# Nine instead of eight feed-forward chunks as seven products, and the sums T1 and T3 of the weights formed by accumulating loads

## The chip, the cores and the metric

The kernel runs on one core of a Trainium2 chip. The metric is the device time of one execution in microseconds. Before the change it is 2186.28 us, the median of three runs (2185.25 to 2186.5).

## The reference

One layer of a hybrid encoder for 256 tokens of width 2048, all in float32:

```
x = LN1(alpha*x + 0.5*(silu(x@w1) * (x@w3)) @ w2)          # feed-forward 1, D_FF = 5632
x = LN2(alpha*x + mixer(x))                                # projections w_in, mLSTM (4 heads), stick-breaking
                                                           # attention (8 heads), two gated up-projections, w_out
x = LN3(alpha*x + 0.5*(silu(x@w1') * (x@w3')) @ w2')       # feed-forward 2
x = x + sigmoid(x@w_ple_gate) * (p@w_ple_proj)
```

The weights are read from HBM in float32, plain loads of 440.87 MB in all; the work is nearly all in the matrix products.

## The kernel before

**Products.** TensorE takes float32 numbers here as a rounded part and a rest, so every weight tile is split: ScalarE casts the raw tile to the rounded part (`split_one`, L1262), VectorE subtracts it from the raw tile to get the rest (L1266). A raw weight tile is 256 rows by 512 columns, [128, 2, 512], 512 KB. A *unit* is one weight tile against one half of the tokens (128): two row groups times three matmuls of 128x512 (L1316, L1317, L1318), six matmuls in one go. A plain product uses each split for two units, one for each half of the tokens.

**Seven products for eight.** `seven` (L348 to L402) computes a 2x2 block product, two token halves and two weight matrices (w1 and w3 of a chunk, or two column ranges of w_in), with seven block products for eight, each against its own combination of weight tiles. For every four row groups i (four sets to a chunk, since D = 2048) there are four raw tiles: b11, b12, b22 and b21. Product 1 uses b11 itself; product 5 uses T1 = b11 + b12; product 7 uses T3 = b12 + b22; products 6 and 4 use T1 + b22 and further + b21, formed in b11's page. So a set has seven splits of one unit each, and four sums. A sum is formed in one of two ways:

- by VectorE, `plus`, L365: one tensor_tensor over [128, 1024];
- by an accumulating load: GpSimd issues a DMA that reads the second tile from HBM and adds it onto the page of the first. For T1 this is `plus_load`, L371, issued as soon as product 1's split of b11 is done (L1268 to L1270). For T3 it stands in `loads()`, L1239: b22 is added onto b12's page when b12 has landed, long before its split; the load of b12 is moved AHEAD = 3 loads forward for it (L1209).

The last argument of `seven` says for which sets T1 and T3 come by loads. Feed-forward chunks have `(range(4), (3,))`: T1 always, T3 in the last set only. The mixer's five double products (`both7`, L412) have `none = ((), ())`: both by VectorE. The sums of products 6 and 4 are VectorE's always.

**Feed-forward** (`ffn`, L562). The 5632 hidden columns are 11 chunks of 512. Chunks 0, 4 and 8 are plain (`up`: gate with w1, hidden with w3, 32 units); the other eight go through `up7` (28 units). The hidden chunks are transposed and split (`transposed`, L289) and go through `down`: w2 for a list of chunks, four column groups, each group ending with one VectorE addition per token half (L641). `weave` (L165) strews the units of the eight seven-product chunks evenly through the main line of plain gate, hidden and down units; the last two chunks' down passes follow as a tail.

**Mixer** (L1021 to L1130). In the same way the five `both7` products are woven into the main line of projections, with the mLSTM and stick-breaking heads (`stick`, L974) hung in by a planner (`Sched`) with fixed delays. The matmuls of a head take a PSUM bank; the first one of `stick` is at L982, and its bank is one that VectorE's L1012 of an earlier head has to leave first.

**Order and buffers.** The order on every engine is fixed when the program is built. All raw tiles, splits, activations and residuals share one pool of PAGES = 48 pages of 4 KB per partition. `HELD` gives, per stage, how many raw tiles may be loaded ahead and how many splits may be held: (8, 6) in the feed-forward and "wide" stages, (6, 6) where the mixer is woven, (5, 6) in the rest of the mixer. Plain loads go over SyncE's queue (L1234), accumulating loads over GpSimd's, each queue in order; a load waits until its page is free, which is mostly when TensorE has used the split that lay there.

Of the kernel before, what the change touches and what calls it, by code (L numbers as in the profile page):

```python
# [16 lines left out]
D = 2048  # L17
# [5 lines left out]
EPS = 1e-5  # L23
COL = 512

PAGES = 48
TEMP_BUFS = 6


HELD = {"ffn": (8, 6), "mix": (5, 6), "woven": (6, 6), "wide": (8, 6)}  # L30
RAW_EDGE, SPLIT_EDGE = 4, 11
EDGE = 6

# [145 lines left out]
def flat(pairs):  # L179
    return [u for p in pairs for u in p]  # L180
# [7 lines left out]
def kernel(  # L188
# [6 lines left out]
    nc = tc.nc  # L195
# [152 lines left out]
    def seven(wa, ca, wb, cb, rows, cols, act, done, loaded):  # L348

        n = rows // (4 * P)
        accs = {m: {} for m in range(1, 8)}
        accs[2] = accs[1]

        def unit(m, i, tile, src, half, sub):
            return Unit(tile, half, accs[m], src, i, sub, i == 0 and m != 2, i == n - 1,  # L360
                        lambda ps, t, m=m: done(m, ps))

        def plus(out, a, b):
            def make():
                nc.vector.tensor_tensor(out=out.tile[:, :, :cols], in0=a.tile[:, :, :cols], in1=b.tile[:, :, :cols],  # L365
                                        op=ALU.add)
            return make

        def plus_load(out, src):
            def make():  # L370
                nc.gpsimd.dma_start(out=out.tile[:, :, :cols], in_=src, accum_op=ALU.add)  # L371
            return make

        one, rest, then = [], [], []
        for i in range(n):
            b11, b12, b22, b21 = (rows_of(w, (4 * i + sub) * P, c, cols)
                                  for w, c, sub in ((wa, ca, 0), (wb, cb, 0), (wb, cb, 2), (wa, ca, 2)))
            m1 = Weight(b11, [b11], [])
            if i in loaded[0]:
                m5 = Weight(b11, [], [], plus_load(b11, b12.src[0]), m1)  # L380
                m1.soon.append(m5)
            else:
                m5 = Weight(b11, [b12], [], plus(b11, b11, b12), m1)
            if i in loaded[1]:
                assert i in loaded[0]
                b12.plus = b22.src
                m7 = Weight(b12, [b12], [b12])
            else:
                m7 = Weight(b12, [b12, b22] if i in loaded[0] else [b22], [b12], plus(b12, b12, b22),
                            m1 if i in loaded[0] else m5)  # L390
            m6 = Weight(b11, [b22] if i in loaded[1] else [], [], plus(b11, b11, b22), m5)
            m2 = Weight(b21, [], [b21])
            m4 = Weight(b11, [b21], [b11], plus(b11, b11, b21), m6)
            one.append(unit(1, i, m1, act, 0, 0))
            rest.append([unit(5, i, m5, act.forms, 0, 0), unit(7, i, m7, act.forms, 1, 0),
                         unit(6, i, m6, act.forms, 0, 2), unit(3, i, Weight(b22, [], [b22]), act.forms, 1, 2)])
            then += [unit(4, i, m4, act, 1, 2), unit(2, i, m2, act, 0, 2)]
            then[-1].onto = True
        first = []
        for i in range(n):  # L400
            first += one[i + 1:i + 2] + rest[i]
        return one[:1], first, then  # L402

    def in_line(pairs):

        out = []
        for head, first, then in pairs:
            at = max(len(out) - 4, 0)
            out = out[:at] + head + out[at:] + first + then
        return out  # L410
# [151 lines left out]
    def ffn(w1, w3, w2, act, norm, skew=True, ahead=()):  # L562
        n = FF // COL
        hT = ActT(act_tile)

        def turn(src, c, t):
            transposed(src, hT, c, t)
            drop()
            return
            yield  # L570

        def up(c):
            s = {}

            def gate(ps, t):
                s[t] = temp()
                activate(s[t][:], ps, ACT.Silu)

            def hidden(ps, t):
                nc.vector.tensor_tensor(out=s[t][:], in0=ps, in1=s[t][:], op=ALU.mult)  # L580
                sched.spaced(turn(s[t], c, t), DELAY["h"] + 2.0 * t, TURN_GAP)

            return group(w1, range(0, D, 2 * P), c * COL, COL, act, gate), group(w3, range(0, D, 2 * P), c * COL, COL, act, hidden)

        def up7(c):
            r, held = {}, {}

            def both(out, a, b, op):
                nc.vector.tensor_tensor(out=out, in0=a, in1=b, op=op)  # L589

            def done(m, ps):
                held[m] = ps
                if m == 1:
                    r["u"] = temp()
                    nc.scalar.copy(r["u"][:], ps)
                elif m == 2:
                    r["g0"] = temp()
                    activate(r["g0"][:], ps, ACT.Silu)
                    sched.spawn(late(r["u"], r["v"], r["z"], r["g0"]), DELAY["late" if c < n - 1 else "last"])
                elif m == 6:  # L600
                    u, v, z = r["u"], temp(), temp()
                    both(u[:], ps, u[:], ALU.add)
                    both(v[:], held[5], u[:], ALU.add)
                    r["v"], r["z"] = v, z
                    sched.spawn(rest(), DELAY["rest"])
                elif m == 4:
                    sched.until(lambda: "rest" in r)
                    both(r["u"][:], ps, r["u"][:], ALU.add)
                    sched.spawn(silu(r["u"]), DELAY["silu"])
                elif m == 3:  # L610
                    both(r["v"][:], ps, r["v"][:], ALU.subtract)

            def rest():
                both(r["u"][:], held[7], r["u"][:], ALU.add)
                both(r["z"][:], held[5], r["u"][:], ALU.add)
                r["rest"] = True
                return
                yield

            def silu(x):  # L620
                activate(x[:], x[:], ACT.Silu)
                return
                yield

            def late(u, v, z, g0):
                both(v[:], v[:], g0[:], ALU.mult)
                nc.vector.scalar_tensor_tensor(out=z[:], in0=z[:], scalar=-1.0, in1=u[:], op0=ALU.mult, op1=ALU.mult)
                drop(2)
                sched.spaced(turn(v, c, 0), DELAY["h"], TURN_GAP)
                sched.spaced(turn(z, c, 1), DELAY["h"] + 2.0, TURN_GAP)  # L630
                return
                yield

            return seven(w1, c * COL, w3, c * COL, D, COL, act, done, (range(4), (3,)))

        def down(*chunks):
            pairs = []
            for g in range(D // COL):
                def add(ps, t, g=g):
                    xs = xres(t, g * COL)  # L640
                    nc.vector.scalar_tensor_tensor(out=xs, in0=ps, scalar=0.5, in1=xs,  # L641
                                                   op0=ALU.mult, op1=ALU.add)
                    if n - 1 in chunks:
                        norm.chunk(t, g)
                pairs += group(w2, [c * COL + r for c in chunks for r in (0, 2 * P)], g * COL, COL, hT, add)
            return pairs

        gate, hidden = zip(*(up(c) for c in (0, 4, 8)))
        program.extend((skewed(gate[0][:SKEW]) if skew else flat(gate[0][:SKEW])) + flat(gate[0][SKEW:]))
        main = flat(hidden[0] + gate[1] + down(0) + hidden[1] + gate[2] + down(1, 2) + hidden[2] + down(3, 4, 5)  # L650
                    + down(6, 8, 7))
        side = in_line([up7(c) for c in (1, 2, 3, 5, 6, 7, 9, 10)])
        program.extend(main[:HEAD] + weave(main[HEAD:], side))
        program.append(norm.load)
        program.extend(ahead)
        tail = down(9) + down(10)
        program.extend(flat(tail[:-SKEW]) + skewed(tail[-SKEW:]))
        boundary("mix")
# [426 lines left out]
            parts.reverse()  # L1085
        return parts[0] + parts[1]

    none = ((), ())

    def gate_dest(g):  # L1090
        def dest(k, t):
# [10 lines left out]
    gate = branch(0, 1)  # L1102
    main = v(0) + v(1) + sb(8, 9, 2, 3) + sb(10, 11, 4, 5) + [Mode("wide")] + sb(12, 13, 6, 7) + sb(14, 15) + [lambda: sched.spawn(lane())] + branch(0, 0) + gate[:4] + bring_ym_back(gate[4:] + ups(0)) + ups(1) + ups(2)
# [112 lines left out]
    def limits(j):  # L1216

        if at_edge(j):
            return RAW_EDGE, SPLIT_EDGE
        return HELD[[m for e, m in modes if e <= j][-1]]  # L1220

# [132 lines left out]
```

## Time and profile before

| | |
|---|---|
| median of three runs | 2186.28 us |
| the profiled execution's own time | 2185.81 us |
| its span in the profile | 2184.1 us |
| granted TensorE clock, mean | 0.998 |
| TensorE busy | 2169.5 us, 99% |
| VectorE busy | 1925.1 us, 88% |
| ScalarE busy | 1331.5 us, 61% |
| GpSimd busy | 97.2 us, 4% |
| DMA queues: plain loads / accumulating loads | 60.9% / 11.4% of 16 engines |

The span is the time from the first to the last instruction of the program in the profile; the execution's own time has 1.7 us more around it. "Busy" counts an engine as busy while any of its instructions runs; since matmuls are pipelined and overlap, a busy TensorE has to be checked against the distance from one matmul to the next. The feed-forward blocks fill the span from about 0 to 670 us and from about 1420 to 2040 us, the mixer lies between them, and the last product follows.

### The profile page before, as it was taken

Reading aid. Unit: us, or ns where it says so; the run is one execution under the profiler, and the core shown is the slowest. Engines: PE = TensorE matmul, PEld = TensorE weight load, DVE = VectorE, ACT = ScalarE, POOL = GpSimd, SP = SyncE. Lnnn points to the kernel's source line nnn. Section 1 sums busy time; section 2 is a strip of 40 time slices with the busy share of each in tenths; the row PEclk is TensorE's granted clock in tenths of the full one; section 3 lists DMA queues with packets and bytes.
Section 4 is the critical chain, followed back from the end, with each engine's and each line's share of the span. In section 5 each row is a group of like instructions: output and inputs, shape, how many; then the busy total and the mean of one; then the engine's idle time right before and its main releaser. Section 6 shows DMA issues by size and latency. Waiting matters only on the chain. (4 is left out here: it accounts for less than half of the span.)

```text
span 2184.1 us, 27443 instructions
## 1 busy us (share of the span) xinstructions
PE 2169.5 (99%) x9846; PEld 1793.3 (82%) x9846; DVE 1925.1 (88%) x2102; ACT 1331.5 (61%) x1632; POOL 97.2 (4%) x88
## 2 busy tenths in 40 slices
PE   9999999999999999999999999999999999999999
PEld 7888888888888887888878888888888888888887
DVE  6899989999988899898888985799999998999874
ACT  6656565656555765677766564555665655665572
POOL 0010000001000000000000000010001000100000
PEclk9999999999999999999999999999999999999999
DMA  8788788778894755564756686578878878888643
GB/s 320 201 246 244 223 240 250 232 222 253 255 295 139 226 175 174 183 202 143 254 160 221 220 284 212 177 189 252 240 222 237 256 213 230 261 258 259 241 166 103
DMA packets 256521, 484.57 MB, mean 222 GB/s; under 512 B 15576, under 2 KB 32896, under 8 KB 256384
## 3 DMA queue, kind: packets, MB, share of 16 engines
q1 hardware_dynamic: 234624, 440.87, 60.9%
q0 software_dynamic: 21760, 41.95, 11.4%
q8 instruction: 77, 1.26, 0.2%
q14 instruction: 60, 0.49, 0.1%
HBM read 476.47 MB, written 6.29 MB: 221 GB/s over the span
## 5 line engine op out<-in xcount | busy, mean ns | idle before, releaser
L1262 ACT CAST split<-raw 128x1024 fp32r<-128x1024 f32 (+2 forms) x1065 | 1072.2, 1044 | 509.4 <-DVE raw L365 206.8
L1266 DVE TENSOR_TENSOR split<-raw,split 128x1024 fp32r<-128x1024 f32 (+2 forms) x1065 | 1251.7, 1209 | 109.5 <-ACT split L1262 99.4
L1316 PE MATMUL mm<-split,actT 128*128 128x512 f32 (+1 forms) x3080 | 1208.3, 392 | 1.4 <-DVE big L417 1.4
L1318 PE MATMUL mm<-split,actT 128*128 128x512 f32 (+1 forms) x3080 | 1194.6, 388 | 0.6 <-DVE actT L299 0.6
L1317 PE MATMUL mm<-split,actT 128*128 128x512 f32 (+1 forms) x3080 | 1193.3, 387 | 1.2 <-DVE split L1266 1.1
L1318 PEld LDWEIGHTS mm<-split,actT 128*128 128x128 f32 x3080 | 578.7, 188 | 122.0 <-DVE actT L299 1.4
L1316 PEld LDWEIGHTS mm<-split,actT 128*128 128x128 f32 x3080 | 579.3, 188 | 116.9 <-issue 2.7
L1317 PEld LDWEIGHTS mm<-split,actT 128*128 128x128 f32 x3080 | 579.4, 188 | 116.0 <-DVE split L1266 2.5
L365 DVE TENSOR_TENSOR raw<-raw 128x1024 f32<-128x1024 f32 x256 | 310.4, 1217 | 5.2 <-DMA raw<-in_ffn_w_dram 4.0
L371 POOL DMA_DIRECT2D raw<-in_ffn_w_dram x64 | 77.9, 1217 | 1689.7 <-DVE split L1266 1575.4
L294 ACT CAST actT<-ms 128x512 fp32r<-128x512 f32 x60 | 35.1, 587 | 95.2 <-PE ms L292 90.1
L242 ACT ACTIVATE temp<-mm 128x512 f32<-128x512 f32 (+1 forms) x38 | 21.6, 575 | 87.5 <-PE mm L1318 87.5
L589 DVE TENSOR_TENSOR temp<-mm,temp 128x512 f32<-128x512 f32 x96 | 65.1, 685 | 6.7 <-PE mm L1318 5.6
L641 DVE SCALAR_TENSOR_TENSOR big<-mm,big 128x512 f32<-128x512 f32 x96 | 65.4, 683 | 5.3 <-PE mm L1318 5.3
L299 DVE TENSOR_TENSOR actT<-ms,actT 128x512 fp32r<-128x512 f32 x60 | 41.1, 687 | 26.7 <-ACT actT L294 16.9
L238 ACT ACT_TABLE_LOAD x34 | 43.6, 1283 | 0.6
L287 DVE TENSOR_TENSOR actT<-temp,actT 128x512 fp32r<-128x512 f32 x40 | 26.5, 687 | 17.3 <-ACT actT L286 17.2
L286 ACT CAST actT<-temp 128x512 fp32r<-128x512 f32 x40 | 24.0, 620 | 8.5 <-DVE temp L310 7.8
L1176 DVE TENSOR_TENSOR temp<-temp,big 128x512 f32<-128x512 f32 (+1 forms) x10 | 5.8, 582 | 25.6 <-ACT temp L242 25.6
L1119 DVE SCALAR_TENSOR_TENSOR big<-big,mm 128x512 f32<-128x512 f32 x8 | 5.5, 686 | 25.3 <-PE mm L1318 25.3
L292 PEld LDWEIGHTS ms<-ident,temp 128*128 128x128 f32 x176 | 21.6, 139 | 7.2 <-PE mm L1318 1.7
L242 ACT ACTIVATE temp<-ms,gbT 128x128 f32<-128x128 f32 x64 | 24.1, 459 | 5.6 <-PE ms L516 5.6
(133 smaller groups left out, 577.6 us busy)
## 6 DMA issues: line engine op xcount, KB each, us to landing
raw<-in_ffn_w_dram SPq DMA_DIRECT2D x527, 512.0 KB, 5.1
raw<-in_w_in_dram SPq DMA_DIRECT2D x144, 512.0 KB, 4.3
raw<-in_ffn_w_dram POOLq DMA_DIRECT2D x80, 512.0 KB, 7.9
raw<-in_w_out_dram SPq DMA_DIRECT2D x32, 512.0 KB, 5.4
raw<-in_w_ple_gate_dram SPq DMA_DIRECT2D x32, 512.0 KB, 4.6
raw<-in_w_in_dram SPq DMA_DIRECT2D x56, 256.0 KB, 3.0
raw<-in_w_up_m_dram SPq DMA_DIRECT2D x16, 512.0 KB, 4.5
raw<-in_w_up_sb_dram SPq DMA_DIRECT2D x16, 512.0 KB, 4.5
```

Source lines behind the costliest of these rows:

```text
L238: nc.scalar.preload_act_table_set(table[0])
L242: nc.scalar.activation(out, in_, func, **kw)
L299: nc.vector.tensor_tensor(out=dst[:, 1], in0=ps[:], in1=dst[:, 0], op=ALU.subtract)
L365: nc.vector.tensor_tensor(out=out.tile[:, :, :cols], in0=a.tile[:, :, :cols], in1=b.tile[:, :, :cols], op=ALU.add)
L371: nc.gpsimd.dma_start(out=out.tile[:, :, :cols], in_=src, accum_op=ALU.add)
L589: nc.vector.tensor_tensor(out=out, in0=a, in1=b, op=op)
L641: nc.vector.scalar_tensor_tensor(out=xs, in0=ps, scalar=0.5, in1=xs, op0=ALU.mult, op1=ALU.add)
L1262: nc.scalar.copy(hi[:, ks], r[:, ks])
L1266: nc.vector.tensor_tensor(out=lo[:, ks], in0=r[:, ks], in1=hi[:, ks], op=ALU.subtract)
L1316: nc.tensor.matmul(ps, hi, w[0][:, k, :u.cols], start=first, stop=False, skip_group_check=u.onto)
L1317: nc.tensor.matmul(ps, hi, w[1][:, k, :u.cols], start=False, stop=False, skip_group_check=u.onto)
L1318: nc.tensor.matmul(ps, lo, w[0][:, k, :u.cols], start=False, stop=last, skip_group_check=u.onto)
```

## The change

- PAGES 48 to 51. The SBUF that is kept for the descriptors of GpSimd's DMA queue is set to 4096 bytes per partition (`dynamic_dma_scratch_size=4096`), where no size was given before.
- HELD: three more raw tiles ahead in "ffn", "woven" and "wide", one more in "mix".
- Feed-forward: chunks 0 and 3 are plain, the other nine go through `up7`; T1 and T3 come by loads in all four sets. The down passes of the main line take chunks (0), (1, 2), (3, 4), (5, 6), (7, 8), where they took (0), (1, 2), (3, 4, 5), (6, 8, 7); (9) and (10) stay in the tail.
- Mixer: T1 and T3 of the five double products come by loads.

From L651 on, the lines of the new kernel are one lower than those of the old.

```diff
-PAGES = 48
+PAGES = 51
 TEMP_BUFS = 6
...
-HELD = {"ffn": (8, 6), "mix": (5, 6), "woven": (6, 6), "wide": (8, 6)}
+HELD = {"ffn": (11, 6), "mix": (6, 6), "woven": (9, 6), "wide": (11, 6)}
...
-            return seven(w1, c * COL, w3, c * COL, D, COL, act, done, (range(4), (3,)))
+            return seven(w1, c * COL, w3, c * COL, D, COL, act, done, (range(4), range(4)))
...
-        gate, hidden = zip(*(up(c) for c in (0, 4, 8)))
+        gate, hidden = zip(*(up(c) for c in (0, 3)))
         program.extend((skewed(gate[0][:SKEW]) if skew else flat(gate[0][:SKEW])) + flat(gate[0][SKEW:]))
-        main = flat(hidden[0] + gate[1] + down(0) + hidden[1] + gate[2] + down(1, 2) + hidden[2] + down(3, 4, 5)
-                    + down(6, 8, 7))
-        side = in_line([up7(c) for c in (1, 2, 3, 5, 6, 7, 9, 10)])
+        main = flat(hidden[0] + gate[1] + down(0) + hidden[1] + down(1, 2) + down(3, 4) + down(5, 6) + down(7, 8))
+        side = in_line([up7(c) for c in (1, 2, 4, 5, 6, 7, 8, 9, 10)])
         program.extend(main[:HEAD] + weave(main[HEAD:], side))
...
-    none = ((), ())
+    none = (range(4), range(4))
...
-    nc = bacc.Bacc("TRN2", target_bir_lowering=False, num_devices=1)
+    nc = bacc.Bacc("TRN2", target_bir_lowering=False, num_devices=1, dynamic_dma_scratch_size=4096)
```

## The prediction

> **What bounds the kernel now.** I read the page's busy line and its 40 slices first, to see whether one engine is busy throughout.
>
> ```profile
> span 2184.1 us, 27443 instructions
> PE 2169.5 (99%) x9846; PEld 1793.3 (82%) x9846; DVE 1925.1 (88%) x2102; ACT 1331.5 (61%) x1632; POOL 97.2 (4%) x88
> PE   9999999999999999999999999999999999999999
> DMA  8788788778894755564756686578878878888643
> ```
>
> TensorE is, with 14.6 us idle in all. Busy is not yet peak, so I looked in the timeline of TensorE for the distance between matmuls, deep in the first feed-forward block; these are the first and the last of 20 in a row.
>
> ```profile
> 299.78 0.39 PE L1317 MATMUL mm<-split,actT 128*128 128x512 f32 x1
> 304.09 0.39 PE L1318 MATMUL mm<-split,actT 128*128 128x512 f32 x1
> ```
>
> 19 steps in 4.31 us: 0.2268 us a matmul, 1.361 us a unit of six. The engine runs at its pace there, and what leaves its program leaves the time, as long as the others keep up. How much room they have, the view by stages shows (columns: stretch, its length, busy us of PE, PEld, DVE, ACT, POOL with counts, granted clock, DMA share, GB/s).
>
> ```profile
> 60.00:640.00 580.00, 579.52 (x2595) 479.62 (x2594) 540.22 (x528) 348.21 (x368) 45.34 (x38) 1.00 0.82 239
> 700.00:1090.00 390.00, 388.79 (x1868) 322.79 (x1867) 348.00 (x465) 273.63 (x425) 0.00 (x0) 1.00 0.60 189
> 1090.00:1160.00 70.00, 66.37 (x285) 53.80 (x284) 54.97 (x60) 46.89 (x57) 0.00 (x0) 0.95 0.55 173
> ```
>
> In the woven feed-forward stage (60 to 640; 1440 to 2020 is alike) VectorE is busy 93% and the DMA engines 0.82, and still TensorE idles 0.48 us in 580. In the mixer it idles: 1.21 us, then 3.63, the latter with a lower granted clock. The timeline shows that place.
>
> ```profile
> 1119.61 1.62 PE L982 MATMUL ms<-big 128*128 128x256 f32 x4 [3.63 <-DVE actT L1012]
> 1121.45 0.63 PE L1317 MATMUL mm<-split,actT 128*128 128x512 f32 x1
> 1121.88 0.63 PE L1318 MATMUL mm<-split,actT 128*128 128x512 f32 x1
> 1115.74 1.05 ACT L1262 CAST split<-raw 128x1024 fp32r<-128x1024 f32 x1 [2.26 <-DVE raw L365]
> 1116.70 0.42 ACT L1010 CAST actT<-ms 128x128 fp32r<-128x128 f32 x2
> 1112.17 2.35 DVE L1266 TENSOR_TENSOR split<-raw,split 128x1024 fp32r<-128x1024 f32 x2
> 1114.44 2.35 DVE L365 TENSOR_TENSOR raw<-raw 128x1024 f32<-128x1024 f32 x2
> 1116.71 2.35 DVE L1266 TENSOR_TENSOR split<-raw,split 128x1024 fp32r<-128x1024 f32 x2
> 1118.98 0.48 DVE L1012 TENSOR_TENSOR actT<-ms,actT 128x128 fp32r<-128x128 f32 x2
> PE mm L1316 <- DVE big L417: 1.4, 1, 1.4
> PE mm L1317 <- DVE split L1266: 1.1, 1, 1.1
> ```
>
> A head's first matmul (L982) waits for VectorE's L1012, which stands behind four splits and two sums of weights (L365); ScalarE's cast L1010 too stands behind a cast that waited for a sum. After 3.63 us of idleness the matmuls go at 0.43 us steps instead of 0.227 for a while: nine of them cost 9 x 0.2 = 1.8 us. The last two rows (from the lists of waits) are the other stops, 1.4 us at 1166 and 1.1 us at 819, again for VectorE. Together, 3.63 + 1.8 + 1.4 + 1.1 = 7.9 us of the mixer are VectorE's lateness.
>
> **The change part by part.** By the counts of the built programs:
>
> *TensorE: a gain of 10.9 us.* A plain chunk is 32 units, one by seven products 28. One chunk more in each block takes 2 x 4 x 6 = 48 matmuls away, 48 x 0.2268 = 10.9 us. Transposes stay.
>
> *VectorE and ScalarE: hidden, if barely, in the feed-forward blocks.* The page has the prices.
>
> ```profile
> L1262 ACT CAST split<-raw 128x1024 fp32r<-128x1024 f32 (+2 forms) x1065 | 1072.2, 1044 | 509.4 <-DVE raw L365 206.8
> L1266 DVE TENSOR_TENSOR split<-raw,split 128x1024 fp32r<-128x1024 f32 (+2 forms) x1065 | 1251.7, 1209 | 109.5 <-ACT split L1262 99.4
> L365 DVE TENSOR_TENSOR raw<-raw 128x1024 f32<-128x1024 f32 x256 | 310.4, 1217 | 5.2 <-DMA raw<-in_ffn_w_dram 4.0
> L589 DVE TENSOR_TENSOR temp<-mm,temp 128x512 f32<-128x512 f32 x96 | 65.1, 685 | 6.7 <-PE mm L1318 5.6
> L641 DVE SCALAR_TENSOR_TENSOR big<-mm,big 128x512 f32<-128x512 f32 x96 | 65.4, 683 | 5.3 <-PE mm L1318 5.3
> ```
>
> Per block: 28 splits for 16 in the chunk that changes, +12 x 1.209 = +14.5 us; sums L365, -24 (T3 of eight chunks) + 8 (products 6 and 4 of the ninth) = -16 x 1.217 = -19.5; combinations of products, 6 more at L589, 2 more of the same size, 2 fewer at L580, +6 x 0.685 = +4.1; one down pass more, 8 x 0.683 = +5.5. Sum +4.6 us. So VectorE's 540.2 of 580 becomes 544.8 of 574.6, 93% to 95%: some 30 us to spare where it had 40. ScalarE gets 12 x 1.044 = +12.5 us and stays near 63%. I put this at nothing; the cover is that splits are made ahead (up to six are held).
>
> *Mixer: a gain of 0 to 7.9 us, I take 3.5.* Here nothing is added to VectorE and 40 sums leave it, 40 x 1.217 = 48.7 us. The order of TensorE's instructions in the mixer does not change at all, that of VectorE only by these sums. Between the two L1012 of the quoted place one L365 of two goes, and one more shortly ahead: L1012 comes 1.2 to 2.4 us earlier, so the 3.63 us stop shrinks to 1.2 to 2.4 us. The other two waits are each about the length of one sum. I take 1.2 + 0.6 + 0.6 for the three and 1.1 for a shorter slow stretch: 3.5 us. The lower end is 0, because the new loads can be late in their turn; the upper is all 7.9.
>
> *DMA: hidden, with less cover.* The window 60 to 640 of the DMA view, and two stretches of 2 us in which only accumulating and only plain loads run:
>
> ```profile
> q1 hardware_dynamic: 61279, 118.15, 61.3%
> q0 software_dynamic: 10336, 19.93, 20.2%
> raw<-in_ffn_w_dram SPq DMA_DIRECT2D x228, 512.0 KB, 5.2
> raw<-in_ffn_w_dram POOLq DMA_DIRECT2D x38, 512.0 KB, 8.1
> 462.00:464.00 2.00, 2.00 (x10) 1.68 (x9) 1.80 (x3) 1.17 (x2) 0.00 (x0) 1.00 1.15 209
> 1276.00:1278.00 2.00, 2.00 (x13) 1.65 (x12) 2.00 (x3) 0.77 (x3) 0.00 (x0) 1.00 1.02 414
> ```
>
> A share above 1 says that the packets' times count waiting on each other. Full capacity is rather 414 GB/s for plain loads, 524 KB / 414 = 1.27 us each, and 209 GB/s for accumulating ones, 2.51 us each. A woven stage has 230 plain loads before and after, and 40 accumulating ones before, 72 after (nine chunks, eight each): (230 x 1.27 + 40 x 2.51) / 580 = 68% becomes (292 + 181) / 574.6 = 82%. By the shares, which are an upper bound, 32 x (20.2% of 580 / 38 = 3.08 us) = 99 us more makes 0.82 x 580 + 99 = 575 of 574.6, full. I take the 82%, since the 2 us stretches show what the engines do when asked; the other end is a rival. In the mixer 40 accumulating loads add 100 us to 460 at a share of 0.6: about 0.8.
>
> *Queues.* GpSimd issues 184 accumulating loads for 80. Their rows:
>
> ```profile
> L371 POOL DMA_DIRECT2D raw<-in_ffn_w_dram x64: 1176/1198/1692, 51.4 to 1983.3; - x64
> DMA to landing us min/median/max: 5.7/8.0/10.6
> ACT split L1262 <- DMA raw<-in_ffn_w_dram: 14.3, 9, 3.2
> ```
>
> Two issues of 1.2 us per set and 16 us leave the queue free. But it is in order: T3's load waits for b12 to land (5.2 us), and a T1 load behind it in the queue waits too. In the built order, 8 to 10 units now lie between a T1 load's issue and the split that needs it (10.9 to 13.6 us), where it was mostly 11 or 12 (15.0 to 16.3). Against that stand 8.0 us, at worst 10.6, plus the issue's own wait: still in time for most, and the third row (window 60 to 640) shows that such waits of ScalarE, 14.3 us in nine, have cost TensorE nothing so far. T3 is needed 17 units or more (23 us) after its plain load is issued: safe. The deeper HELD is paid by the three pages and only issues loads earlier; SyncE's queue has as many loads as before (897 instructions in both). I put all this at nothing, with a loss of 0 to 5 us as its ends.
>
> A rule of the Trainium skill speaks against the change: "SBUF — State Buffer", section "SBUF: two separate sides", says that a DMA issued by GpSimd is starved of its descriptors while VectorE runs an instruction on both of its ports, and gives 620 ns against 3100 ns. This trace disagrees so far: with VectorE busy 93% the issues take 1176 to 1692 ns, never two times the least. By the rule a T1 load would be some 2 us later (an estimate from its figures).
>
> **Sum.** Against the profiled execution's 2185.81 us (span 2184.1 and 1.7 around it): 2185.8 - 10.9 - 3.5 = 2171.4. The median of the runs is 0.5 above that execution, so 2172.
>
> **Rivals.**
>
> *1. Only the matmuls count (2175 to 2181.9).* The mixer's stops stay, because ScalarE or the heads' delays and not the sums set them, or the feed-forward loses up to 5 us. Without the mixer 2186.3 - 10.9 = 2175.4; with it and a loss of 5, 2180. For it: the mixer idled for other reasons too; against it: in all three stops the releaser is VectorE.
>
> *2. Late T1 loads starve TensorE (slower).* Place: the four sets of each woven chunk, 72 in both blocks. A T1 load that lands too late stops ScalarE at its cast, then VectorE. VectorE's spare is 30 us over 36 sets, 0.83 us a set; that is the point from which it decides. If T1 is later, so that VectorE idles 1.3 us a set, TensorE loses 72 x 0.5 = 34 us: 2186 - 11 + 34 = 2209; at 2 us a set 72 x 1.17 = 84, 2259. For it: the DMA's upper bound, the shorter distance, two accumulating loads following each other; against it: capacity by the 2 us stretches, and 14.3 us of such waits so far. The skill's starved descriptors would act in this way.
>
> *3. The same lateness just eats the gain (2182 to 2190.6).*
>
> *4. The change doing something else than it says* I leave out: the built program has the 48 matmuls fewer and the 104 accumulating loads more.
>
> **How the numbers follow.** About 4.4 us, 0.2%, is what a measurement of this kernel tells from no change. My forecast (2167 to 2176, around 2172) gets 0.53, rival 1 with its upper part (2176 to 2181.9) 0.15, rival 3 0.08, rival 2 0.24. So faster by over 0.2%: 0.68; the same: 0.08; slower: 0.24. The range takes in the whole mixer gain, 2186.3 - 10.9 - 7.9 = 2167.5, and reaches up through rivals 1 and 3 and the mildest of rival 2: 2167 to 2192, which leaves out about 2 in 10.
>
> **What would show it.** Right: 48 matmuls fewer at the same 0.227 us step, TensorE idle under 1 us in each woven stage, VectorE near 95% there, DMA share 0.9 or more, the wait of L982 for L1012 under 2.5 us and no 0.43 us steps after it. Wrong: waits of TensorE for L1266 or ScalarE's L1262 for accumulating loads in the woven stages by the hundred us (rival 2), or the stop at L982 unchanged (rival 1). GpSimd issues well above 1.7 us would mean the descriptors.

## The result and the profile after

| | before | after |
|---|---|---|
| median of the runs compared | 2186.39 us | 2246.25 us |
| ratio, 95% interval | | 1.0276, 1.0264 to 1.0288 |
| span of the profiled execution | 2184.1 us | 2240.6 us |
| TensorE not busy in the span | 14.6 us | 58.4 us |

The change makes the kernel 60 us slower; the forecast was 14 us faster. From the page of the new kernel, the lines that answer to those of before: the span, the busy line, TensorE's and the DMA engines' slices, the shares of the chain, four groups, and the accumulating loads' time to landing (last column, median us):

```profile
span 2240.6 us, 27706 instructions
PE 2182.2 (97%) x9798; PEld 1782.8 (80%) x9798; DVE 1884.2 (84%) x2082; ACT 1344.5 (60%) x1658; POOL 222.8 (10%) x192
PE   9999999999999999999999999999999999999999
DMA  9899889998996587978998976779988999889742
PE 70%; DMA 16%; DVE 7%; issue 4%; ACT 2%; POOL 0%; SPq 0%; POOLq 0%; DVEq 0%; ACTq 0%
L1265 DVE TENSOR_TENSOR split<-raw,split 128x1024 fp32r<-128x1024 f32 (+1 forms) x1089 | 1277.2, 1211 | 227.2 <-ACT split L1261 222.5
L1261 ACT CAST split<-raw 128x1024 fp32r<-128x1024 f32 (+1 forms) x1089 | 1086.0, 1043 | 583.7 <-DMA raw<-in_ffn_w_dram 213.4
L365 DVE TENSOR_TENSOR raw<-raw 128x1024 f32<-128x1024 f32 x184 | 224.4, 1220 | 1.6
L641 DVE SCALAR_TENSOR_TENSOR big<-mm,big 128x512 f32<-128x512 f32 x112 | 76.5, 684 | 3.4 <-PE mm L1317 3.3
raw<-in_ffn_w_dram POOLq DMA_DIRECT2D x144, 512.0 KB, 9.2
```

TensorE has its 48 matmuls fewer (9798 for 9846), and no engine is busier than the forecast said. Yet the chain that ended last goes through DMAs for 16% of the span (the page of before, which follows its chain over about half the span, has no DMA in it), and ScalarE's casts stand 213.4 us waiting for loads. Nothing is slower in itself: a cast is 1.04 us, a split's rest and a sum 1.21 and 1.22, as before. The view by stages says where the time is lost (stretch, length, busy us of PE, PEld, DVE, ACT, POOL, clock, DMA share, GB/s):

```profile
60.00:640.00 580.00, 556.79 (x2430) 450.10 (x2429) 509.86 (x506) 337.14 (x362) 78.94 (x66) 0.99 0.92 251
1440.00:2020.00 580.00, 558.72 (x2452) 452.08 (x2451) 516.45 (x524) 335.21 (x362) 80.64 (x67) 1.00 0.91 250
```

TensorE idles 23 us here, where it idled 0.5, and VectorE, which should have come to 95%, fell to 88%: it is not too busy, it waits. From the first matmul against a weight's rest (L1317 before, L1316 after) in one stage to that in the next, and in the last column to the last such matmul, the trace gives these stage times in us, the frame for all that follows:

| | block 1 | mixer | block 2 | rest |
|---|---|---|---|---|
| before | 691.7 | 688.3 | 690.6 | 100.1 |
| by the forecast (-5.45, -3.5, -5.45, 0) | 686.2 | 684.8 | 685.2 | 100.1 |
| after | 723.3 | 684.6 | 718.8 | 100.1 |

The mixer is as forecast in its sum. The two blocks are 37.1 and 33.6 us above it, 71 us over 72 sets, 1 us a set.

The list of waits (us in total, times, longest) names the chain:

```profile
ACT split L1261 <- DMA raw<-in_ffn_w_dram: 213.4, 50, 13.2
DVE split L1265 <- ACT split L1261: 222.5, 117, 9.2
PEld mm L1316 <- DVE split L1265: 44.7, 51, 2.3
PE mm L1316 <- DVE split L1265: 25.2, 33, 1.8
PE ms L981 <- DVE actT L1011: 0.4, 1, 0.4
```

A load is late, ScalarE stands before its cast, VectorE before the rest of the split, then TensorE. Before, the last row was 3.6 us, and the first was:

```profile
ACT split L1262 <- DMA raw<-in_ffn_w_dram: 45.4, 21, 8.7
```

Nearly all the late loads are T1's: nobody waits for a T3 load in the blocks. The T1 loads themselves, by their line (issues' duration in ns, minimum, median and maximum; then the time to landing):

```profile
L371 POOL DMA_DIRECT2D raw<-in_ffn_w_dram x72: 1178/1208/2157, 56.6 to 2046.9; - x72
DMA to landing us min/median/max: 5.8/9.7/13.5
```

And one place in the timeline, two sets of one chunk. L1238 is a T3 load's issue, L371 a T1 load's:

```profile
260.21 1.20 POOL L1238 DMA_DIRECT2D raw<-in_ffn_w_dram  x1 [11.40 <-DVE raw L365]
260.94 1.69 POOL L371 DMA_DIRECT2D raw<-in_ffn_w_dram  x1
274.20 1.20 POOL L1238 DMA_DIRECT2D raw<-in_ffn_w_dram  x1 [11.57 <-DMA raw<-in_ffn_w_dram]
274.93 1.69 POOL L371 DMA_DIRECT2D raw<-in_ffn_w_dram  x1
273.39 2.94 ACT L1261 CAST split<-raw 128x1024 fp32r<-128x1024 f32 x3 [8.12 <-DMA raw<-in_ffn_w_dram]
285.93 2.00 ACT L1261 CAST split<-raw 128x1024 fp32r<-128x1024 f32 x2 [3.86 <-DMA raw<-in_ffn_w_dram]
274.47 1.23 DVE L1265 TENSOR_TENSOR split<-raw,split 128x1024 fp32r<-128x1024 f32 x1 [7.57 <-ACT split L1261]
274.49 0.49 PE L1315 MATMUL mm<-split,actT 128*128 128x512 f32 x1 [0.79 <-ACT split L1261]
275.75 0.50 PE L1316 MATMUL mm<-split,actT 128*128 128x512 f32 x1 [0.77 <-DVE split L1265]
291.77 0.50 PE L1316 MATMUL mm<-split,actT 128*128 128x512 f32 x1 [1.82 <-DVE split L1265]
```

Read it from the left column. At 260.21 GpSimd issues a T3 load, after 11.40 us in which it stood before it, and 0.7 us later a T1 load that had been allowed since 257.8, when product 1's split was done. That T1 lands at 273.3, 12.4 us after its issue; ScalarE has then stood 8.12 us and VectorE 7.57. The next T1 load was allowed from 266.9 on, but the T3 load ahead of it in GpSimd's queue waits for its own b12 to land, until 274.20: 8.0 us in the queue, then 10.9 to landing (285.9). The splits held ahead pay for most of either lateness, TensorE for the last 1.6 and 1.8 us.

In the two woven stretches (1160 us) the starts of the units' matmuls, with 0.1 us taken off for each transpose in between, show how it adds up: 45 distances of more than 0.8 us, where before had two, are 50 us above the normal pace, and 46 between 0.4 and 0.8 us, where before had none, 11 us more.

### The profile page after: what moved, and what is told of

Same layout as the page of the kernel before. It is cut to its first block, busy times and chain, and to the rows that moved or that the text cites. A ratio compares the mean times of both kernels' runs of the same rounds, so it can differ in the third digit from the quotient of the medians.

```text
span 2240.6 us, 27706 instructions
## 1 busy us (share of the span) xinstructions
PE 2182.2 (97%) x9798; PEld 1782.8 (80%) x9798; DVE 1884.2 (84%) x2082; ACT 1344.5 (60%) x1658; POOL 222.8 (10%) x192
## 4 chain that ended last, share of the span: by engine, by line
PE 70%; DMA 16%; DVE 7%; issue 4%; ACT 2%; POOL 0%; SPq 0%; POOLq 0%; DVEq 0%; ACTq 0%
PE mm L1316 22%; PE mm L1315 22%; PE mm L1317 22%; DMA raw<-in_ffn_w_dram 15%; DVE split L1265 4%; ACT split L1261 1%; PE ms L292 1%; DVE raw L365 1%; DMA raw<-in_w_in_dram 1%; PE ms L516 0%; DVE temp L589 0%; POOL raw L1238 0%; DVE actT L299 0%; DVE big L641 0%; DVE temp L627 0%
## 5 line engine op out<-in xcount | busy, mean ns | idle before, releaser
L1265 DVE TENSOR_TENSOR split<-raw,split 128x1024 fp32r<-128x1024 f32 (+1 forms) x1089 | 1277.2, 1211 | 227.2 <-ACT split L1261 222.5
L1261 ACT CAST split<-raw 128x1024 fp32r<-128x1024 f32 (+1 forms) x1089 | 1086.0, 1043 | 583.7 <-DMA raw<-in_ffn_w_dram 213.4
L1316 PE MATMUL mm<-split,actT 128*128 128x512 f32 x3064 | 1194.9, 390 | 25.7 <-DVE split L1265 25.2
L1315 PE MATMUL mm<-split,actT 128*128 128x512 f32 x3064 | 1205.3, 393 | 6.8 <-ACT split L1261 4.4
L1317 PE MATMUL mm<-split,actT 128*128 128x512 f32 x3064 | 1190.5, 389 | 0.6 <-DVE actT L299 0.6
L1316 PEld LDWEIGHTS mm<-split,actT 128*128 128x128 f32 x3064 | 577.7, 189 | 156.6 <-DVE split L1265 44.7
L1317 PEld LDWEIGHTS mm<-split,actT 128*128 128x128 f32 x3064 | 577.3, 188 | 120.2 <-DVE actT L299 1.5
L365 DVE TENSOR_TENSOR raw<-raw 128x1024 f32<-128x1024 f32 x184 | 224.4, 1220 | 1.6
L1238 POOL DMA_DIRECT2D raw<-in_ffn_w_dram x72 | 87.2, 1211 | 950.1 <-DMA raw<-in_ffn_w_dram 294.7
L371 POOL DMA_DIRECT2D raw<-in_ffn_w_dram x72 | 100.7, 1412 | 321.1 <-DVE split L1265 300.3
L641 DVE SCALAR_TENSOR_TENSOR big<-mm,big 128x512 f32<-128x512 f32 x112 | 76.5, 684 | 3.4 <-PE mm L1317 3.3
L589 DVE TENSOR_TENSOR temp<-mm,temp 128x512 f32<-128x512 f32 x108 | 73.1, 686 | 1.2
L1238 POOL DMA_DIRECT2D raw<-in_w_in_dram x20 | 23.8, 1189 | 429.9 <-DMA raw<-in_w_in_dram 309.7
L299 DVE TENSOR_TENSOR actT<-ms,actT 128x512 fp32r<-128x512 f32 x60 | 40.9, 685 | 12.2 <-ACT big L298 9.1
L292 PE MATMUL ms<-ident,temp 128*128 128x128 f32 x176 | 27.4, 278 | 15.1 <-DVE actT L299 12.2
L371 POOL DMA_DIRECT2D raw<-in_w_in_dram x20 | 25.0, 1248 | 79.0 <-DVE split L1265 58.9
```

The source lines that it names most:

```text
L292: nc.tensor.transpose(ps[:, k], src[:, k * P:(k + 1) * P], ident[:])
L1238: nc.gpsimd.dma_start(out=r.tile[:, :, :r.cols], in_=r.plus[0], accum_op=ALU.add)
L1261: nc.scalar.copy(hi[:, ks], r[:, ks])
L1265: nc.vector.tensor_tensor(out=lo[:, ks], in0=r[:, ks], in1=hi[:, ks], op=ALU.subtract)
L1315: nc.tensor.matmul(ps, hi, w[0][:, k, :u.cols], start=first, stop=False, skip_group_check=u.onto)
L1316: nc.tensor.matmul(ps, hi, w[1][:, k, :u.cols], start=False, stop=False, skip_group_check=u.onto)
```

## The experiments

Three theories went in. **Q**: T1 loads are late because T3 loads stand directly ahead of them, in GpSimd's queue or in the transfers. **D**: the DMA engines as a whole are full (share 0.92), and whatever is last is late. **V**: VectorE at some 95% has no slack for the blocks in their new form. "T1 lateness" below is worked out from the trace for each T1 load of the blocks: from the end of product 1's rest to the load's issue (queue) and from there to its landing.

### e1_t3_back: the ninth chunk stays, T3 by a load in the last set only

```diff
-            return seven(w1, c * COL, w3, c * COL, D, COL, act, done, (range(4), range(4)))
+            return seven(w1, c * COL, w3, c * COL, D, COL, act, done, (range(4), (3,)))
```

> The changed kernel, but T3 in the feed-forward blocks comes by a load in the last set of a chunk only, as before; nine chunks, 51 pages and the mixer's loads stay. Theory Q (the T1 loads of a chunk's first two sets are late because they stand behind T3's loads, in GpSimd's queue and on the DMA rings): the two blocks get back what they lost, 2186.4 - 10.9 - 3.7 = 2172, 2169 to 2177. Theory D (the DMA engines as a whole are full at a share of 0.92): the same, since the accumulating loads fall from 72 to 45 a block. Theory V (VectorE at 95% is what starves TensorE): 27 more sums a block put VectorE near 100%, so 2200 or more.

Measured: 2180.69 us, ratio 0.998 (0.9971 to 0.9989). 66 us of the loss go with 27 T3 loads per block. But the time is 9 us above the number of theories Q and D, and far below that of V. Its first woven stretch, in the columns of the stages above:

```profile
60.00:640.00 580.00, 576.16 (x2575) 475.17 (x2574) 569.99 (x563) 356.26 (x381) 50.19 (x42) 1.00 0.86 243
```

The 27 sums are back on VectorE, which is busy 98% of 580 us. So T3's loads are what costs, and without them something smaller is left.

### e2_t3_behind: the same loads, T3 behind T1

Each T3 load is held back in GpSimd's program until behind the next T1 load, or until its own tile is due.

```diff
-                nc.gpsimd.dma_start(out=r.tile[:, :, :r.cols], in_=r.plus[0], accum_op=ALU.add)
+                held_back.append((r, r.tile))
...
+        if w.soon:
+            put_plus()
```

> The changed kernel with all its loads, but GpSimd issues each T3 load behind the next T1 load instead of ahead of it (it is held back until then, or until its tile is due). Bytes, sums and splits are the same. Theory Q: the T1 loads go out within 0.6 us of their split and land first; most of the loss goes, 2172 to 2195. Theory D: same bytes in the same time, so 2235 to 2255 stays.

Measured: 2186.92 us, ratio 1.0005 (0.9996 to 1.0014). Its first woven stretch, and from its list of waits ScalarE's for loads:

```profile
60.00:640.00 580.00, 575.08 (x2570) 474.30 (x2569) 539.29 (x533) 352.65 (x380) 80.75 (x67) 1.00 0.95 265
```

```profile
ACT split L1270 <- DMA raw<-in_ffn_w_dram: 173.3, 80, 8.5
```

The same bytes in another order are 59 us faster, at a DMA share of 0.95, higher than in the slow kernel. That ends D: the share was no sign of a limit. The order is what counts. ScalarE still waits 173 us for loads, T3 now among them, but no single wait is over 8.5 us. The kernel stays 15 us above the forecast of 2172: set 1's T1 still takes 12.2 us to land (median), with a held T3 load 7.7 us ahead of it.

### e3_eight_t3 and e4_mixer_only: the parts alone

e3 keeps the eight chunks and down passes of before, with T3 by loads in all sets, the new pages and the mixer's loads. e4 leaves the feed-forward as it was and takes only pages, HELD, descriptor space and the mixer's loads.

Against the new kernel:

```diff
 e3 and e4:
-        gate, hidden = zip(*(up(c) for c in (0, 3)))
+        gate, hidden = zip(*(up(c) for c in (0, 4, 8)))
-        main = flat(hidden[0] + gate[1] + down(0) + hidden[1] + down(1, 2) + down(3, 4) + down(5, 6) + down(7, 8))
-        side = in_line([up7(c) for c in (1, 2, 4, 5, 6, 7, 8, 9, 10)])
+        main = flat(hidden[0] + gate[1] + down(0) + hidden[1] + gate[2] + down(1, 2) + hidden[2] + down(3, 4, 5)
+                    + down(6, 8, 7))
+        side = in_line([up7(c) for c in (1, 2, 3, 5, 6, 7, 9, 10)])
 e4 alone:
-            return seven(w1, c * COL, w3, c * COL, D, COL, act, done, (range(4), range(4)))
+            return seven(w1, c * COL, w3, c * COL, D, COL, act, done, (range(4), (3,)))
```

> Eight chunks by seven products and the down passes as before, but T3 by loads in all sets, with 51 pages, the new HELD and the mixer's loads. Theories Q and D: the loss is T3's loads, eight ninths of it, so 2186.4 - 3.7 + 62 = 2245, 2230 to 2255. If the ninth chunk and the down passes in pairs are what starves TensorE: 2183.

> The feed-forward blocks as before (eight chunks, T3 by a load in the last set only), with 51 pages, the new HELD, the smaller descriptor space and T1 and T3 of the mixer by loads. If the mixer's gain of 3.7 us between the two profiles is VectorE's relief: 2182.7, 2181 to 2184, with the stop at the head's first matmul under 1 us. If pages, HELD or descriptor space cost or gain something in the feed-forward blocks, it shows there alone: 2186 and above, or below 2180.

Measured: e3 2211.75 us, ratio 1.0121 (1.0108 to 1.0135); e4 2182.46 us, ratio 0.9986 (0.9977 to 0.9995). e4's stages are 692.7, 683.7 and 690.6: three pages more, deeper HELD and 4096 bytes for descriptors cost nothing worth naming in the blocks, and the mixer alone gives 4.6 us. e3 fell between its two numbers: T3's loads cost 28 us (707.5 and 702.9 against 691.7 and 690.6) without any ninth chunk, so the other 43 come only with it (e1, the ninth chunk without these loads, is 9 us above its number). That nine chunks on a shorter main line leave a T1 load less time (8 to 10 units where it was 11 or 12) fits the sums of T1's lateness further down, but no run changes this distance alone.

### f1_swap, f2_t3_03_swap, f3_behind_swap: products 5 and 7 exchanged

Product 7 before product 5 in each set gives a T1 load one or two units more until its split. The exchange was put on e1, on T3 by loads in sets 0 and 3, and on e2.

```diff
-            rest.append([unit(5, i, m5, act.forms, 0, 0), unit(7, i, m7, act.forms, 1, 0),
+            rest.append([unit(7, i, m7, act.forms, 1, 0), unit(5, i, m5, act.forms, 0, 0),
```

> The kernel of the run with T3 back on VectorE, with products 5 and 7 exchanged in each set, so that the split of T1 comes one place later and its load has some 2 us more. That run is 9 us above the 2171.4 that the matmuls and the mixer alone would give. Theory Q (T1 loads late): ScalarE's waits for accumulating loads, 83 us there, fall under 30 us and the time to 2172 to 2177. Theory V (VectorE at 98% in the woven stages): nothing moves, 2179 to 2182.

> Nine chunks, T3 by loads in sets 0 and 3 of a chunk (the two whose T3 load stands well away from a T1 load in GpSimd's queue), products 5 and 7 exchanged, the mixer by loads. VectorE has 18 sums a block less than with T3 back on it in three sets, 96% instead of 98%. Theory Q: like the run without T3 in set 0, 2172 to 2177. Theory V: lower than that run, 2171 to 2175, and by itself the step that helps.

> T3's load issued behind the next T1 load, all four sets, and products 5 and 7 exchanged. Without the exchange 2186.9, with ScalarE waiting 173 us for accumulating loads. Theory Q: T1 in time now, 2174 to 2182, unless T3, needed one place sooner, is late in its turn (20 of 72 waited before): then 2185 or more. Theory D (DMA share 0.95 stretches all): 2185 or more, with both kinds late.

Measured: f1 2226.17 us, ratio 1.0187 (1.017 to 1.0204); f2 2203.69, 1.0078 (1.0063 to 1.0093); f3 2257.57, 1.0323 (1.0308 to 1.0339). f1 and f2 missed all their numbers, upward; f3 lies far into an open end, 2185 or more. From f1's waits in the first woven stretch, and that stretch itself:

```profile
ACT split L1261 <- DVE raw L365: 193.3, 82, 6.4
DVE split L1265 <- ACT split L1261: 26.1, 25, 1.2
```

```profile
60.00:640.00 580.00, 557.73 (x2468) 456.70 (x2467) 546.82 (x538) 336.42 (x363) 51.22 (x43) 0.99 0.83 232
```

ScalarE hardly waits for T1 loads any more (2.7 us in 6 waits in the whole span, where it was 86.6 us in 35 in e1); a longer wait for VectorE took their place. Products 5 and 6 use the same page b11, and now stand next to each other: VectorE takes the rest of T1, then forms the sum for 6 in the same page, ScalarE casts it, VectorE takes that rest. In e1 that first row was 104.6 us in 59 waits. So these kernels do not test T1's lateness cleanly. They do show how little VectorE can stand idle: its work here is that of e1, 570 us in 580 there; it idles 33 us of 580, and TensorE 22.

### f4_t3_half and h3_t3_eighth: the queue stays, the transfer shrinks

f4 adds the first of T3's two row groups, h3 128 columns of it, in the blocks and the mixer; the rest of T3 is left out of the computation, so these two kernels are probes and no versions to use:

```diff
-                nc.gpsimd.dma_start(out=r.tile[:, :, :r.cols], in_=r.plus[0], accum_op=ALU.add)
 f4, for tiles of 512 columns:
+                nc.gpsimd.dma_start(out=r.tile[:, 0:1, :r.cols], in_=r.plus[0][:, 0:1], accum_op=ALU.add)
 h3:
+                nc.gpsimd.dma_start(out=r.tile[:, 0:1, 0:128], in_=r.plus[0][:, 0:1, 0:128], accum_op=ALU.add)
```

> The changed kernel, with each T3 load adding only the first of the two row groups of its tile (half the bytes; the second half of T3 is left out of the computation). The queue's order and what it waits for stay. If the loss is the waiting of T1's issue behind T3's wait for b12, most of it stays: 2225 to 2245, with issue delays of 3 to 8 us in sets 0 and 1. If it is T3's transfer on the DMA rings ahead of T1's, most of it goes: 2190 to 2220, T1's landing near 9 us.

> The new kernel with each T3 load adding only 128 of the 512 columns of the first of the two row groups (an eighth of its bytes; the rest of T3 is left out). T3's loads stand in GpSimd's queue at the same places and still wait there for b12. With half the bytes set 1's T1 loads still waited 3.7 us in the queue, landed 2 us sooner, and the time was 2187.8. If the transfer in front is what the harm needs, 2171 to 2180 us, with T1 landing in 8 to 9 us; if the wait in the queue alone does it, 2188 or more.

Measured: f4 2187.75 us, ratio 1.0005 (0.9996 to 1.0015); h3 2170.82, ratio 0.9928 (0.9912 to 0.9944). f4 is just under its lower range, that of the transfer, and h3 at the low end of its own. Of h3, the same place in the timeline, the T1 loads' time to landing, and the two stretches:

```profile
259.56 0.90 POOL L1239 DMA_DIRECT2D raw<-in_ffn_w_dram  x1 [10.86 <-DMA raw<-in_ffn_w_dram]
260.19 1.50 POOL L371 DMA_DIRECT2D raw<-in_ffn_w_dram  x1
```

```profile
DMA to landing us min/median/max: 5.8/8.0/10.4
```

```profile
60.00:640.00 580.00, 579.32 (x2594) 479.36 (x2593) 547.81 (x541) 359.27 (x385) 69.12 (x66) 1.00 0.86 241
1440.00:2020.00 580.00, 580.00 (x2594) 480.00 (x2593) 550.61 (x541) 359.63 (x382) 69.17 (x66) 1.00 0.87 247
```

GpSimd's queue is as it was: the T3 load waits 10.86 us for b12, the T1 load goes out 0.6 us behind it. But there is nearly nothing to transfer ahead of it, it lands after 7.5 us, and TensorE idles 0.7 us in 1160. This kernel takes 2170.8 us. The forecast of the whole change, 2172, is what the change costs without T3's transfers.

### g2_ahead6: T3's loads issued earlier

```diff
-AHEAD = 3
+AHEAD = 6
```

> The new kernel with b12 loaded 6 instead of 3 loads ahead, so that T3's loads are issued earlier against T1's; the same bytes, the same T1 loads. If what costs the 71 us is a T3 transfer just in front of a T1 transfer, this gives back a good part: 2175 to 2215 us. If the DMA engines as a whole are too full, it stays at 2235 or more.

Measured: 2255.47 us, ratio 1.032 (1.0303 to 1.0337). That is what D foretold, and D was already out by e2; the timeline shows why nothing was given back:

```profile
276.45 1.19 POOL L1238 DMA_DIRECT2D raw<-in_ffn_w_dram  x1 [8.49 <-DMA raw<-in_ffn_w_dram]
277.18 1.69 POOL L371 DMA_DIRECT2D raw<-in_ffn_w_dram  x1
281.21 1.19 POOL L371 DMA_DIRECT2D raw<-in_ffn_w_dram  x1 [2.34 <-DVE split L1265]
```

A T3 load that is earlier in the program need not be earlier in time, since it waits for its b12 (here 8.49 us), and one still stands directly ahead of set 1's T1: set 0's T1 goes free, set 1's lands after 12.4 us, and the one behind after 12.3.

### g1_t3_03, h1_t3_023, h2_t3_023_held, g3_mixed: which sets

g1 has T3 by loads in sets 0 and 3, h1 in 0, 2 and 3. h2 is h1 with set 2's T3 held back as in e2; g3 is the new kernel with those of sets 1 and 2 held back.

```diff
-            return seven(w1, c * COL, w3, c * COL, D, COL, act, done, (range(4), range(4)))
 g1:
+            return seven(w1, c * COL, w3, c * COL, D, COL, act, done, (range(4), (0, 3)))
 h1 and h2:
+            return seven(w1, c * COL, w3, c * COL, D, COL, act, done, (range(4), (0, 2, 3)))
 h2 (g3: i in (1, 2)):
-                b12.plus = b22.src
+                b12.plus, b12.late = b22.src, i == 2
...
+                if r.late:
+                    held_back.append((r, r.tile))
```

> The new kernel with T3 by loads in the first and the last set of a chunk only (products in their old order), 18 sums more on VectorE per block than in the new kernel, 9 fewer than with T3 in the last set alone. If T1 loads are late only where a T3 load stands directly in front of them, and VectorE at 98% was what kept the version with the last set alone at 2180.7 us instead of 2171.4, this one is 2172 to 2179. If any second T3 load per chunk already makes T1 loads late, it loses its share of the 71 us, a third or so: 2195 to 2210.

> The new kernel with the T3 loads of sets 1 and 2 held back in GpSimd's order until behind the next T1 load, those of sets 0 and 3 issued at once; the same bytes. Holding back all of them gave 2186.9 us, with ScalarE then waiting for T3 loads 20 times and T1 loads mostly in time. If what is left there (15 us above 2171.4) is late T3 loads that were held back without need, this is 2172 to 2184. If what is left is that two accumulating loads overlap in either order, it stays at 2184 to 2200.

> T3 by loads in sets 0, 2 and 3, all issued at once: of the two pairs of the new kernel in which a T1 load goes out 0.7 us behind a T3 load, the one in set 0 (behind set 1's T3) is gone, that in set 1 (behind set 2's T3; there 5.1 us in GpSimd's queue and 11.7 us to landing, 16.8 from product 1's split) is kept. If any T1 load that takes over some 13 us, queue and landing together, stops TensorE, this one still loses in one set per chunk: 2195 to 2250 us. If set 1's T1 was late only because set 0's was late before it, it is 2172 to 2180.

> The same three T3 loads per chunk, the one of set 2 held back in GpSimd's order until behind set 1's T1 load; the same bytes as in the kernel with sets 0, 2 and 3 at once. If the order of the two decides, no T1 load takes 13 us, VectorE has 11 us per block less than with sets 0 and 3, and it is 2171 to 2180 us. If three T3 loads per chunk are too many for the queue in any order, it is as the one with all at once, 2195 or more.

Measured: g1 2176.06 us, ratio 0.9957 (0.9942 to 0.9972); h1 2190.82, 1.0023 (1.0013 to 1.0033); h2 2183.67, 0.9989 (0.9979 to 0.9999); g3 2231.44, 1.021 (1.0195 to 1.0225). g1 came out as Q said and beats both kernels. Its busy line and its first woven stretch:

```profile
PE 2158.9 (99%) x9798; PEld 1783.1 (82%) x9798; DVE 1924.6 (89%) x2118; ACT 1347.7 (62%) x1658; POOL 179.8 (8%) x156
```

```profile
60.00:640.00 580.00, 578.76 (x2591) 478.64 (x2590) 565.20 (x558) 359.07 (x384) 59.82 (x50) 1.00 0.89 252
```

h1, with one bad pair left in each chunk, loses 15 us against g1, just under the low end of what was said; turning that pair round (h2) gives half of it back and ends between its two numbers. g3 missed: the held load of set 2 and the next one now fall together ahead of set 2's T1 load.

```profile
271.33 1.20 POOL L1241 DMA_DIRECT2D raw<-in_ffn_w_dram  x1 [4.29 <-DMA raw<-in_ffn_w_dram]
272.06 1.69 POOL L371 DMA_DIRECT2D raw<-in_ffn_w_dram  x1
```

At 265.9 the held T3 load had gone out, at 271.33 that of set 3, once its b12 was there, and the T1 load right behind lands after 12.2 us. Holding a load back moves the collision to another T1 load, unless there is room for it.

The T1 loads of these kernels, medians of 18 (before: 16) in us, queue + landing = sum:

| | set 0 | set 1 | set 2 | time |
|---|---|---|---|---|
| before | 0.3 + 8.8 = 9.1 | 0.3 + 7.8 = 8.1 | 0.3 + 7.7 = 8.0 | 2186.4 |
| h3, an eighth of T3 | 0.4 + 9.3 = 9.6 | 3.0 + 7.6 = 10.2 | 0.3 + 8.2 = 8.5 | 2170.8 |
| g1, T3 in 0 and 3 | 0.4 + 8.8 = 9.1 | 0.4 + 8.8 = 9.1 | 0.4 + 9.8 = 10.5 | 2176.1 |
| e2, T3 behind T1 | 0.4 + 8.8 = 9.2 | 0.4 + 12.2 = 12.6 | 0.4 + 9.2 = 9.5 | 2186.9 |
| h2, T3 in 0, 2, 3, 2 held back | 0.4 + 8.8 = 9.1 | 0.4 + 8.5 = 8.9 | 2.2 + 10.8 = 13.0 | 2183.7 |
| f4, half of T3 | 0.4 + 10.3 = 10.9 | 3.7 + 9.7 = 13.5 | 0.3 + 8.3 = 8.6 | 2187.8 |
| h1, T3 in 0, 2, 3 | 0.4 + 8.9 = 9.4 | 2.5 + 10.9 = 13.6 | 0.4 + 11.2 = 11.8 | 2190.8 |
| g3, 1 and 2 held back | 0.4 + 9.1 = 9.4 | 0.4 + 9.3 = 9.6 | 3.1 + 11.7 = 15.1 | 2231.4 |
| after | 1.5 + 12.0 = 13.6 | 5.1 + 11.7 = 16.8 | 0.4 + 9.6 = 9.9 | 2246.3 |
| g2, AHEAD 6 | 0.4 + 9.3 = 9.6 | 5.8 + 11.6 = 17.1 | 0.4 + 9.8 = 10.2 | 2255.5 |

(Each column is a median by itself, so a sum can be 0.2 off.) Up to a sum of some 11 us a T1 load costs little. Against h3's two blocks (18 chunks) a chunk loses 0.8 us in h2 (13.0 in one set), 0.9 in e2 (12.6, and some T3 loads late), 1.0 in f4 and 1.4 in h1 (13.5), 3.1 in g3 (15.1), 3.9 in the new kernel (13.6 and 16.8) and 4.7 in g2 (17.1). That g2 with one late set loses more than the new kernel with two, these sums do not explain. The budget from the built order was 8 to 10 units, 10.9 to 13.6 us. Where it is 11 or 12 units, 15.0 to 16.3 us, more is borne: in e4 a T3 load goes out 0.7 us ahead of set 2's T1 too, the sum there is 12.4, and the blocks are as before; in e3 it is 15.8 in set 2, and a chunk loses 1.8 us.

## Why the prediction was wrong, step by step

**TensorE, -10.9 us: right.** 48 matmuls fewer, and where nothing is late the pace is the same (20 matmuls in a row of the new kernel, first and last: 19 steps in 4.32 us, 0.227 each). h3 comes to 2170.8, so the gain is there to be had.

```profile
299.62 0.39 PE L1316 MATMUL mm<-split,actT 128*128 128x512 f32 x1
303.94 0.39 PE L1317 MATMUL mm<-split,actT 128*128 128x512 f32 x1
```

**VectorE, hidden: right for the change as made.** h3 has the new kernel's VectorE work at full speed: 547.8 and 550.6 of 580, against 544.8 of 574.6 forecast, and loses nothing by it. Beyond it the cover thins: g1 at 565 of 580 is 5 us above h3, e1 at 570 is 10 us above. That VectorE is the cause there is likely, not shown; h2 at 550 is above h3 as well, by 13 us, with T1 loads of set 2 that take 10.8 us to land.

**Mixer, -3.5 us: the number right, in part by luck.** 688.3 to 684.6 is -3.7, and e4 alone gives -4.6. The stop at a head's first matmul went from 3.6 to 0.4 us, further than the 1.2 to 2.4 expected, and the slow steps behind it are gone; of the other two stops, one is gone and one went from 1.4 to 1.2. Against that stands a stop that was not there before:

```profile
839.68 1.04 ACT L1261 CAST split<-raw 128x1024 fp32r<-128x1024 f32 x1 [5.89 <-DMA raw<-in_w_in_dram]
841.26 1.39 PE L799 MATMUL ms<-ident,temp 128*128 128x128 f32 x4 [2.46 <-ACT temp L787]
```

The mixer's first T1 load lands 7.6 us after its issue (832.03). ScalarE stands 5.89 us before its cast, the copy of L787 behind the cast comes late, and TensorE waits 2.46 us for it. The sum named late loads only as the reason of its lower end, 0. The mixer's other T1 loads stop TensorE nowhere: medians of 0.4 us in the queue, 8.7 to landing, and 14.9 us from product 1's rest to the cast that needs T1.

**DMA, capacity: right, and no help.** The share rose to 0.92 as the list of signs had it, and e2 runs 59 us faster at 0.95. A share near full says neither that the engines limit nor that a single load is in time.

**Queues: the step that failed.** The text saw it: "T3's load waits for b12 to land (5.2 us), and a T1 load behind it in the queue waits too", and against 10.9 to 13.6 us it set "8.0 us, at worst 10.6, plus the issue's own wait: still in time for most", "I put all this at nothing". Two sizes were wrong. The landing of 8.0 us was that of accumulating loads with little directly ahead of them; 0.7 us behind another it is 12. And the wait in the queue was read as short, where it is 5.1 us in set 1, because b12 is not always loaded when the queue comes to it: against the 5.2 us of the forecast, T3's issue follows that of b12's load after 8.8 us in set 1 and 10.5 in set 2 (medians, 0.6 of it after the landing). The positions of T3's loads against T1's were in the built order: nearly every T1 load of sets 0, 1 and 2 has a T3 load directly ahead, and in 28 of the 36 sets 0 and 1 the two go out within 1 us. The units from T1's issue to its split were counted, but the two rows of loads were not laid on top of each other. So the term put at nothing, 0 to 5 us at its ends, measured 71.

The transfer is the part that the harm needs (h3: the wait stays at 3.0 us in set 1, the loss goes). The wait in the queue adds to it: e2, with 12.2 to landing and no such wait, loses 0.9 us a chunk, not 3.9. h3's wait is itself 2 us shorter than the new kernel's. Its b12 is not loaded earlier for that (6.0 us before T1 may go out, 6.4 in the new kernel), but T3 can follow it after 8.2 us instead of 10.5: with less of T3 to move, b12's own load lands sooner. How the 71 us divide between the two can't be told: to keep the transfer and take the wait away T3 would need a page of its own, which was not tried.

Rival 2, "late T1 loads starve TensorE", named the place and the chain, and its prices, 2209 for 1.3 us of VectorE idle in a set and 2259 for 2 us, enclose the 2246 (VectorE idles 70 us over the 33 sets of the first woven stretch, some 2 us each). What spoke against it, and kept its chance at 0.24, was capacity in the 2 us stretches and the waits of a kernel in which the two loads seldom met; neither tells of the order in one queue.

**The rule on starved descriptors** (the Trainium skill, "SBUF — State Buffer", section "SBUF: two separate sides") did not become the cause. The section states it for a VectorE instruction in a 2-port mode and measured it with `tensor_copy`; VectorE's work here is mostly `tensor_tensor` (L1265 and L365 alone are 1501.6 of its 1884.2 us), so the prediction stretched it. In the new kernel some T1 issues take up to 2157 ns, with VectorE less busy than before; in e1, with VectorE busy 98%, the same 72 take at most 1687:

```profile
L371 POOL DMA_DIRECT2D raw<-in_ffn_w_dram x72: 1176/1198/1687, 51.3 to 1986.3; - x72
```

The long ones are those issued right behind another load, as the 1.69 us in the timeline above. e2 shows it best: 1.2 to 1.3 us alone, 1.5 to 1.7 behind one load, 2.0 to 2.2 behind two, 3.2 behind four. A rule that does bear on the case is in the Trainium skill, "DMA: Bandwidth & Descriptors", section "Two DMAs through the same engine are not ordered": within one queue of one DMA engine, descriptors start in order. The landings agree: 12.0 and 11.7 us behind a full T3 load (sets 0 and 1 of the new kernel), 10.3 and 9.7 behind half of one (f4), 9.3 and 7.6 behind an eighth (h3). They do not show the rule by itself, since two loads that share the DMA engines in any other way would also delay each other.

## What to carry to other kernels

When a load that can wait and a load that is urgent share one queue in order, write both out in the order of the built program and look at which stands directly ahead of which; a median landing from a trace in which they seldom met says nothing of it. Add queue wait and landing for the urgent load and set the sum against the distance to its use, set by set, not as a mean: here, with 10.9 to 13.6 us to the use, sums of 10 us cost nothing, 13 to 13.5 about one us a chunk, 15 three and 17 nearly five. And giving up some of the moved work can be the best version: T3 by loads in two sets of four (g1, with the ninth chunk) is 10 us faster than before, in four sets 60 us slower.

## What was not expected of the hardware

- An accumulating load of 512 KB issued 0.7 us behind another lands after some 12 us, where it lands after 7 to 9 when none is close ahead (medians: new kernel, sets 0 and 3, 12.0 and 7.0; before, set 0, 8.8).
- GpSimd's issue of an accumulating load takes 1.2 us alone and about half a us more for each load issued directly before it (e2: 1.5 to 1.7 behind one, 2.0 to 2.2 behind two, 3.2 behind four).
- The same bytes in another order raised the DMA share from 0.92 to 0.95 and took 59 us off the time.
- The space for the descriptors of GpSimd's DMAs set to 4096 bytes per partition cost nothing that shows (e4: 692.7 and 690.6 us in the blocks against 691.7 and 690.6).
